# Three decoder blocks on one core: the first mixture's entry is reordered, V rows and table rows of the third mixer move to GpSimd's DMA queue, and the MLA heads are woven another way

## The chip, the cores and the metric

The program runs on one core of a Trainium2 chip. The metric is device time in microseconds (us) of one execution. The median of three runs of the kernel before is the time that a change is measured against. Engines are named as in the profile: PE (TensorE matmul) and PEld (its weight load), DVE (VectorE), ACT (ScalarE), POOL (GpSimd), SP (SyncE). A name with a q (ACTq, POOLq, SPq) is the sequencer of that engine, which issues DMAs in program order.

## The reference

Three blocks follow one another on 512 tokens of width 1024, in fp32. Cut to the parts that the change touches:

```python
def first_block(...):                      # block 1
    mem_n = rms_norm(mem, mem_norm)
    h = h + hybrid_mixer(rms_norm(h, mix_norm), ...)
    h = h + memory_cross_attention(rms_norm(h, cross_norm), mem_n, ...)
    h = h + hierarchical_moe(rms_norm(h, moe_norm), ...)   # 16 experts, top 2
...
def hierarchical_moe(h, w_rg, b_rg, w_re, b_re, w_e_gate, w_e_up, w_e_down):
    g_prob = jax.nn.softmax((hf @ w_rg) + b_rg, axis=-1)
    grp = jnp.argmax(g_prob, axis=-1)
    e_logits = ((hf @ w_re) + b_re).reshape(N, N_GROUPS, EXPERTS_PER_GROUP)
    ...
    top_p, top_i = lax.top_k(jax.nn.softmax(e_logits, axis=-1), TOP_K)
    ...
    u = jax.nn.silu(xb @ w_e_gate[e]) * (xb @ w_e_up[e])     # each expert's own rows
    return u @ w_e_down[e]
```

Block 2 (its own mixer and a mixture of 16 wide experts) lies in the middle of the time and is not touched. Block 3's mixer runs two attentions on one input: a neighbourhood attention of 8 heads of 64 (scores over a window of the 2D grid plus a table of relative positions, softmax, values) and a latent attention (MLA) of 8 heads (scores 512 by 512 of width 96, softmax, values of width 64), then mixes both with gates.

## The kernel before

One core does everything; activations sit transposed in SBUF as a high and a low part, and every dense product takes three matmuls (high by high, high by low, low by high). Weights come from HBM by SP's queue as tiles named `raw`; for each 128 by 512 slice ACT casts the high part `wh` (line 227) and DVE subtracts it to give the low part `wl` (line 230). A Tile layer records the program and places the instructions of each engine in one order; within an engine nothing overtakes, DMA issues included.

**First mixture's entry (block 1).** The last projection of the cross attention ends with four row tiles (`moe1_tile`): sums of squares, `power` (DVE makes `pw_v`, line 215; POOL raises it to the power -1/2, line 216), transposes into `gate` tiles, a small router product (line 912) and the logits `L` (DVE, line 922). `moe1_route` turns the logits into expert lists on DVE: some thirty small operations on tiles `rt`, a cast to bf16 (line 971), count matmuls (lines 975 to 978), then for chunks of experts a one-hot `oh` (line 992), matmuls (line 997) and `token_rows` (lines 1075 to 1078), whose last cast is the integer index. POOL gathers the rows `xe` of each expert with an indirect DMA (line 1132); PE transposes them (line 1088), ACT and DVE split them into `xeh` and `xel`, and the expert's products begin (line 1103). Beside this stand two pieces for block 2: `mem2_keep`, four POOL adds (line 1247), and `mem2_v` for its second half, 48 products (line 428) with eight `wl`.

**Entry of the third mixer.** `dense_tiles` makes V (matmuls of line 376); `ev_v` copies each row tile out of PSUM (DVE, tile `nv`, line 1810) and stores it to DRAM `vd` with a DMA on ACT's queue (line 1811). Then `dense` makes q and k (matmuls of line 428). Eight loads bring V back in windows `vw` (line 1830), and two loads for each pair of heads bring table rows `rv` (line 1839), all on ACT's queue. The neighbourhood attention that follows has scores (1862), softmax, transposes (442) and values (1876).

**MLA heads.** `mla_part(hp, qt)` is one pair of heads and one tile of queries: two scores (line 1968), softmax on DVE and ACT (maximum 462 or 465, exponential 477, reciprocal 482, scale 485), eight transposes (442) with one copy by DVE (445) and one by ACT (447) into `eT`, sixteen value matmuls (1980, in pairs of the two heads) and a copy (1984). Head pair 0 runs earlier; pairs 1 to 3 are run by `stagger(..., 2)`, which keeps two parts open.

```python
self.together([lambda kt=kt, b=b: values(kt, b) for kt in range(4) for b in (1, 0)])
...
stagger((mla_part(hp, qt) for hp in range(1, 4) for qt in range(4)), 2)
```

## Time and profile before

| what | value |
|---|---|
| median of 3 runs | 3352.58 us (3346.15 to 3354.76) |
| profiled execution | 3355.08 us |
| its span | 3353.2 us |
| mean granted TensorE clock | 0.983 |
| busy PE, DVE, ACT, POOL | 3168.3, 1632.4, 1291.2, 130.9 us |

The profile is of one execution. Its span is the time from the first to the last recorded instruction; 1.9 us lie around it. In a timeline row the columns are start, duration, engine, line, operation, tile written from tile read, and count; the bracket at the end is the idle time of that engine just before the row and what ended it. The granted clock (PEclk) is a share of full speed.

### The profile page before, as it was taken

The page shows a single profiled execution, that of the slowest core. Times are in us where ns is not written, and L with a number is a line of the kernel's source. Part 1 is how long each engine was busy: PE and PEld are TensorE (multiplying, and loading weights), DVE is VectorE, ACT ScalarE, POOL GpSimd, SP SyncE. Part 2 cuts the span into 40 slices and gives each one's busy share as a digit, 9 for nine tenths or more (in the row PEclk, how much of TensorE's full clock was granted, in tenths as well). Part 3 has the DMA queues.
Part 4 walks back from the last instruction along what each step waited for, and adds up shares of the span by engine and source line. Part 5 has one row for each costly group of instructions (what it writes and reads, how often), then busy time and mean ns, then how long its engine had stood idle before and what let it go on. Part 6 is the DMA issues. An engine that isn't in the chain of part 4 may idle for free.

```text
span 3353.2 us, 41283 instructions
## 1 busy us (share of the span) xinstructions
PE 3168.3 (94%) x15456; PEld 2062.4 (62%) x15456; DVE 1632.4 (49%) x3520; ACT 1291.2 (39%) x2662; POOL 130.9 (4%) x128
## 2 busy tenths in 40 slices
PE   8999989998989999999999999899888999999998
PEld 6778766667758777677534333322225685788886
DVE  5557799987364444856211111011105546573356
ACT  6335568876354354654000000000003444452244
POOL 0010110001000000000000000000000000000000
PEclk9999989999999999999899999999999999999999
DMA  5115489975112122125799999999995220132243
GB/s 174 67 66 157 173 305 382 370 282 177 63 38 88 63 66 88 39 89 199 315 420 426 427 427 427 427 427 427 427 427 205 72 95 26 63 114 90 81 170 138
DMA packets 196554, 713.96 MB, mean 213 GB/s; under 512 B 20144, under 2 KB 28096, under 8 KB 147584
## 3 DMA queue, kind: packets, MB, share of 16 engines
q1 hardware_dynamic: 173888, 668.38, 51.4%
q10 hardware_dynamic: 19520, 32.43, 3.1%
q0 software_dynamic: 2944, 10.49, 1.0%
q8 instruction: 123, 2.02, 0.2%
q14 instruction: 79, 0.65, 0.1%
HBM read 693.68 MB, written 17.56 MB: 212 GB/s over the span
## 4 chain that ended last, share of the span: by engine, by line
PE 69%; DMA 15%; DVE 8%; ACT 4%; issue 2%; POOL 1%; ACTq 0%; POOLq 0%; SPq 0%; DVEq 0%
PE acc L428 23%; PE acc L291 7%; PE acc L1701 6%; PE acc L1103 5%; PE acc L1295 5%; DMA xl<-in_w_exp_up_dram 3%; DMA rawx<-in_w_exp_gate_dram 3%; PE acc L1738 3%; PE acc L1125 3%; DMA rawx<-in_w_exp_down_dram 2%; DMA xl<-in_w_exp_down_dram 2%; PE sc L1664 2%; PE acc L376 2%; PE pst L442 2%; DVE wl L230 2%
## 5 line engine op out<-in xcount | busy, mean ns | idle before, releaser
L230 DVE TENSOR_TENSOR wl<-raw,wh 128x512 fp32r<-128x512 f32 (+3 forms) x910 | 606.0, 682 | 578.6 <-ACT wh L227 528.9
L227 ACT CAST wh<-raw 128x512 fp32r<-128x512 f32 (+3 forms) x910 | 546.5, 612 | 717.1 <-PE acc L428 475.1
L428 PE MATMUL acc<-xh,wh 128*128 128x512 f32 x1072 | 426.5, 398 | 7.2 <-ACT wh L227 5.2
L428 PE MATMUL acc<-xl,wh 128*128 128x512 f32 x1072 | 424.5, 396 | 0.0
L428 PE MATMUL acc<-xh,wl 128*128 128x512 f32 x1072 | 423.1, 395 | 0.0
L1701 PE MATMUL acc<-rawx,xe 128*64 128x512 f32 x1256 | 293.1, 601 | 28.1 <-DMA rawx<-in_w_exp_up_dram 20.4
L428 PEld LDWEIGHTS acc<-xh,wh 128*128 128x128 f32 x1072 | 202.4, 189 | 57.1 <-ACT wh L227 7.8
L428 PEld LDWEIGHTS acc<-xh,wl 128*128 128x128 f32 x1072 | 202.5, 189 | 47.0 <-issue 6.7
L428 PEld LDWEIGHTS acc<-xl,wh 128*128 128x128 f32 x1072 | 202.7, 189 | 44.2 <-issue 5.6
L1701 PEld LDWEIGHTS acc<-rawx,xe 128*64 128x64 f32 x1256 | 84.4, 137 | 227.5 <-issue 149.8
L1738 PE MATMUL acc<-rawx,wh 128*64 128x512 f32 x640 | 145.9, 598 | 10.6 <-DMA rawx<-in_w_exp_down_dram 10.6
L291 PE MATMUL acc<-wl,xsh 128*128 128x512 f32 x336 | 133.8, 398 | 4.8 <-DVE wl L230 4.7
L216 POOL TENSOR_TENSOR pw_r<-pw_v,halfneg 128x1 f32<-128x1 f32 (+2 forms) x64 | 59.1, 924 | 2008.2 <-DVE pw_v L215 1990.6
L291 PE MATMUL acc<-wh,xsl 128*128 128x512 f32 x336 | 132.9, 396 | 0.0
L291 PE MATMUL acc<-wh,xsh 128*128 128x512 f32 x336 | 128.9, 392 | 0.0
L1701 PE MATMUL acc<-raw,xe 128*64 128x512 f32 x512 | 118.5, 597 | 8.4 <-DMA raw<-in_w_exp_gate_dram 8.4
L1720 DVE SCALAR_TENSOR_TENSOR wl<-wl,acc 128x512 f32<-128x512 f32 x32 | 22.0, 687 | 203.6 <-PE acc L1701 203.6
L1727 ACT COPY wh<-pst 128x512 f32<-128x512 f32 x32 | 18.8, 586 | 259.8 <-PE pst L1726 259.7
L477 ACT ACTIVATE e<-e,smx 128x512 f32<-128x512 f32 (+3 forms) x160 | 98.9, 619 | 50.2 <-DVE smx L475 36.4
L1103 PE MATMUL acc<-wh,xeh 128*96 128x512 f32 x256 | 103.7, 406 | 0.7 <-ACT xeh L227 0.7
L1738 PEld LDWEIGHTS acc<-rawx,wh 128*64 128x64 f32 x640 | 42.7, 136 | 99.2 <-issue 70.7
L1103 PE MATMUL acc<-wl,xeh 128*96 128x512 f32 x256 | 103.5, 404 | 0.1
(537 smaller groups left out, 5475.1 us busy)
## 6 DMA issues: line engine op xcount, KB each, us to landing
rawx<-in_w_exp_up_dram SPq DMA_DIRECT2D x80, 1024.0 KB
rawx<-in_w_exp_down_dram SPq DMA_DIRECT2D x80, 1024.0 KB
rawx<-in_w_exp_gate_dram SPq DMA_DIRECT2D x77, 1024.0 KB
raw<-in_w_in_dram SPq DMA_DIRECT2D x58, 1024.0 KB
raw<-in_w_exp_gate_dram SPq DMA_DIRECT2D x34, 1024.0 KB
raw<-in_w_exp_down_dram SPq DMA_DIRECT2D x32, 1024.0 KB
raw<-in_w_exp_up_dram SPq DMA_DIRECT2D x30, 1024.0 KB
raw<-in_w_ffn_out_dram SPq DMA_DIRECT2D x22, 1024.0 KB
```

The lines of the kernel that those rows point to most:

```text
L227: nc.scalar.copy(hi, src)
L230: nc.vector.tensor_sub(lo, src, hi.bitcast(F32))
L291: nc.tensor.matmul(acc[a, hf], l[:, js], r, start=(k == 0 and q == 0), stop=(k == nk - 1 and q == 2))
L376: self.nc.tensor.matmul(acc[a], l[:, k, js], r[:, :n], start=(k == 0 and q == 0), stop=(k == nk - 1 and q == 2))
L428: nc.tensor.matmul(outs[j], l, r, start=(kk == 0 and q == 0), stop=(kk == nk - 1 and q == 2))
L442: nc.tensor.transpose(pt[:, k * P:(k + 1) * P], src[:, (b + k) * P:(b + k + 1) * P], self.ident)
L477: nc.scalar.activation(es[i], src[i], AF.Exp, bias=nm[:, i:i + 1], scale=sc[i], accum_out=l[:, i:i + 1])
L1103: nc.tensor.matmul(ps, l[:, k], r, start=(k == 0 and q == 0), stop=(k == 7 and q == 2))
L1125: nc.tensor.matmul(py[hf], l[:, k], r, start=(k == 0 and q == 0), stop=(k == 3 and q == 2))
L1295: nc.tensor.matmul(acc[j], l[:, js], r, start=(k == 0 and q == 0), stop=(k == nk - 1 and q == 2))
L1701: nc.tensor.matmul(acc[f // 2][f % 2 * 64:(f % 2 + 1) * 64], cur[:, k, es], raw[f], start=(k == 0), stop=(k == 7))
L1738: nc.tensor.matmul(py[hf * 64:(hf + 1) * 64], uT[ab][:, kk, c * 64:(c + 1) * 64], raw[:, d, hf * 512:(hf + 1) * 512], start=(i + d == 0), ...
```

## The change

Three places change.

1. *First mixture's entry.* `moe1_route` becomes a generator that stops behind its second chunk of indices; `mem2_v` calls it after its fourth slice. `mem2_keep` and `mem2_v` are placed behind the last row tile's `pw_v` and power. The index chunks become (0,1), (1,4), (4,8), (8,12), (12,16), with the second one-hot behind the first index's cast; `keep_busy` adds 15 matmuls of 128 by 512 in bf16 behind the chunks.
2. *Entry of the third mixer.* V's row tiles are staged in tiles `ne` and `neT`; the stores `vd`, the loads `vw` and `rv` are issued by POOL (`nc.gpsimd`) and no longer by ACT. The weight loads of V, q and k are raised to the front; those of k go to a tile `m` of the merge.
3. *MLA heads.* `mla_part` yields once more, and `weave` replaces `stagger`.

```diff
+    def keep_busy(self, ps, b, n, behind):
+        with self.tc.issue_after(behind):
+            for _ in range(n):
+                self.nc.tensor.matmul(ps, b, b.unsqueeze(1).to_broadcast([P, 4, P]), start=True, stop=True)
...
-        for e0, e1 in ((0,2),(2,5),(5,8),(8,12),(12,16)):
+        done = None
+        busy = self.acc()
+        for e0, e1 in ((0, 1), (1, 4), (4, 8), (8, 12), (12, 16)):
+            if e0 == 4:
+                yield
             n = e1 - e0
             oh = self.XS.tile([P, 4, 4, C], BF, name="oh", bufs=2)
...
+            with tc.issue_after(done) if e0 == 1 else ExitStack():
+                nc.vector.tensor_tensor(oh[:, :, :n], ...)
...
+            if e0:
+                self.keep_busy(busy, self.onesb, 3 if e1 < 16 else 6, mm.ins)
+            done = self.token_rows(self.idx[:C, e0:e1], ...)
...
         def ev_v(a, ps):
-            t = N.tile([P, 512], F32, name="nv")
+            t = (N.tile([P, 2, 256], F32, name="ne", bufs=2).rearrange("p i k -> p (i k)") if a % 2 else
+                 N.tile([P, 4, P], F32, name="neT", bufs=2).rearrange("p k t -> p (k t)"))
             nc.vector.tensor_copy(t, ps)
-            nc.scalar.dma_start(vd[a * P:(a + 1) * P, :], t)
+            nc.gpsimd.dma_start(vd[a * P:(a + 1) * P, :], t)
...
+        raws = {c: [self.raw_group(W, kg, 4, c, 512) for kg in (0, 4)] for c in (1024, 0)}
+        for kg in (0, 4):
+            nc.sync.dma_start(room[:, kg:kg + 4], W[kg * P:(kg + 4) * P, 512:1024].rearrange("(g p) n -> p g n", p=P))
...
-                nc.scalar.dma_start(t, bass.AP(tensor=o.tensor, offset=o.offset, ap=[[64 * 512, 4], [512, 32], [1, 512]]))
+                nc.gpsimd.dma_start(t, bass.AP(tensor=o.tensor, offset=o.offset, ap=[[64 * 512, 4], [512, 32], [1, 512]]))
...
-                nc.scalar.dma_start(rv, bass.AP(tensor=rpb.tensor, offset=rpb.offset + (2 * hp + hh) * 945,
+                nc.gpsimd.dma_start(rv, bass.AP(tensor=rpb.tensor, offset=rpb.offset + (2 * hp + hh) * 945,
...
+            scores(0)
+            yield
+            with behind():
+                last[0] = scores(1).ins
             e = H.tile([P, 2, S], F32, name="e", bufs=3)
...
+                last[0] = self.transposes(eT[:, b], e[:, b], 4, eng="a" if b else "v")
+            yield
             po = self.pst() if hp == 0 else self.acc()
...
+            with behind():
+                self.together([lambda kt=kt, b=b: values(kt, b) for kt in range(4) for b in (1, 0)])
...
+        def weave(parts, depth, tied):
+            open_ = []
+            for g in parts:
+                o = open_.pop(0) if len(open_) == depth else None
+                next(g)
+                last[1] = tied and o is not None
+                if o is None or not tied:
+                    next(g)
+                if o is not None:
+                    next(o)
+                    if tied:
+                        next(g)
+                    next(o, None)
+                open_.append(g)
...
-        stagger((mla_part(hp, qt) for hp in range(1, 4) for qt in range(4)), 2)
+        weave([mla_part(hp, qt) for hp in range(1, 4) for qt in range(4)], 2, True)
...
-            self.moe1_route()
-            self.mem2_keep(*m[0])
-            self.mem2_v(*m[0], (1,))
+            last = self.last_power
+            route = self.moe1_route()
+            with tc.issue_after(last[0]), tc.issue_after(last[1]):
+                self.mem2_keep(*m[0])
+                self.mem2_v(*m[0], (1,), lambda: next(route))
+            next(route, None)
```

**Place 1 in the order of DVE.** Before, the last row tiles and the start of the routing: `xs_3863` belongs to the last row tile, `L_2933` is written once for each row tile, and `rt` opens the routing.

```order
L901 TENSOR_TENSOR xs_3863<-h_2450,grow_3551 128x512
L922 SCALAR_TENSOR_TENSOR L_2933<-sc_3889,pw_r_3856,rb_2912 128x20
L230 TENSOR_TENSOR wl_4165<-raw_4152,wh_4164 128x512
L445 COPY gate_3873<-pst_3874 128x512
L230 TENSOR_TENSOR wl_4175<-raw_4152,wh_4174 128x512
L230 TENSOR_TENSOR wl_4185<-raw_4152,wh_4184 128x512
L230 TENSOR_TENSOR wl_4197<-raw_4194,wh_4196 128x512
L215 TENSOR_SCALAR pw_v_3883<-ss_3880 128x1
L230 TENSOR_TENSOR wl_4207<-raw_4194,wh_4206 128x512
L922 SCALAR_TENSOR_TENSOR L_2933<-sc_3899,pw_r_3884,rb_2912 128x20
```

The same place of the changed kernel, where line 221 is the old 215, 932 the old 922 and 237 the old 230:

```order
L221 TENSOR_SCALAR pw_v_3855<-ss_3852 128x1
L911 TENSOR_TENSOR xs_3863<-h_2450,grow_3551 128x512 x2
L454 COPY gate_3845<-pst_3846 128x512
L221 TENSOR_SCALAR pw_v_3883<-ss_3880 128x1
L237 TENSOR_TENSOR wl_3923<-raw_3920,wh_3922 128x512
L237 TENSOR_TENSOR wl_3933<-raw_3920,wh_3932 128x512
L454 COPY gate_3873<-pst_3874 128x512
L932 SCALAR_TENSOR_TENSOR L_2933<-sc_3889,pw_r_3856,rb_2912 128x20
L237 TENSOR_TENSOR wl_3943<-raw_3920,wh_3942 128x512
L237 TENSOR_TENSOR wl_3953<-raw_3920,wh_3952 128x512
L932 SCALAR_TENSOR_TENSOR L_2933<-sc_3899,pw_r_3884,rb_2912 128x20
```

The last `pw_v` moved ahead of four `wl`; four more `wl`, which stood ahead of it or at the end, now stand inside the routing chain behind the last `L`. On POOL the four adds of line 1247 stood ahead of the last power and now stand behind it.

**Place 2 in the orders of ACT and POOL.** Before, on ACT, the casts of q's weights (`wh` from `raw`) and the DMA issues among them:

```order
L227 CAST wh_19083<-raw_19033 128x512
L1811 DMA vd_18779<-nv_19014 128x512
L1830 DMA vw20_19317<-vd_18779 128x1x512
L227 CAST wh_19101<-raw_19099 128x512
L1830 DMA vw30_19321<-vd_18779 128x1x512
L1830 DMA vw01_19311<-vd_18779 128x1x512
L1830 DMA vw11_19315<-vd_18779 128x1x512
L227 CAST wh_19117<-raw_19099 128x512
L1830 DMA vw21_19319<-vd_18779 128x1x512
L1830 DMA vw31_19323<-vd_18779 128x1x512
L1839 DMA rv_19443<-in_na_rpb_3_dram 128x1x489
L227 CAST wh_19133<-raw_19099 128x512
```

In the changed kernel they stand on POOL, in this row (the two powers are those of the last two row tiles of the norm ahead of the mixer):

```order
L1864 DMA rv_19341<-in_na_rpb_3_dram 128x1x489
L222 TENSOR_TENSOR pw_r_18752<-pw_v_18751,halfneg_83 128x1
L222 TENSOR_TENSOR pw_r_18774<-pw_v_18773,halfneg_83 128x1
L1832 DMA vd_18795<-neT_18906 128x512
L1832 DMA vd_18795<-ne_18909 128x512
L1855 DMA vw00_19316<-vd_18795 128x1x512
L1855 DMA vw10_19320<-vd_18795 128x1x512
L1855 DMA vw20_19324<-vd_18795 128x1x512
L1855 DMA vw30_19328<-vd_18795 128x1x512
L1832 DMA vd_18795<-neT_18969 128x512
L1832 DMA vd_18795<-ne_19029 128x512
L1855 DMA vw01_19318<-vd_18795 128x1x512
```

Three more `vw` and six `rv` follow there; ACT's casts stand in a row with no DMA between them. Two `rv` stand between the powers of the second and the third row tile.

**Place 3 in the order of PE.** Before, two parts of head pair 2 (`sc` or two `acc` hold scores, `acc` with `eT` values):

```order
L442 MATMUL pst_21293<-c_ident_81,e_21183 128x128 x4
L442 MATMUL pst_21299<-c_ident_81,e_21183 128x128 x4
L1980 MATMUL acc_21305<-eT_21292,mv_20099 64x128
L1968 MATMUL acc_21315<-mkT_21264,mqT_21257 128x512
L1980 MATMUL acc_21305<-eT_21292,mv_20099 64x128 x7
L1968 MATMUL acc_21316<-mkT_21278,mqT_21271 128x512
L442 MATMUL pst_21330<-c_ident_81,e_21219 128x128 x4
L442 MATMUL pst_21336<-c_ident_81,e_21219 128x128 x4
L1968 MATMUL sc_21352<-mkT_21264,mqT_21257 128x512
L1980 MATMUL acc_21342<-eT_21329,mv_20099 64x128 x8
L1968 MATMUL sc_21352<-mkT_21278,mqT_21271 128x512
```

The same parts in the changed kernel (line 451 is the old 442, 1994 the old 1968, 2012 the old 1980):

```order
L451 MATMUL pst_21290<-c_ident_81,e_21203 128x128 x4
L451 MATMUL pst_21296<-c_ident_81,e_21203 128x128 x4
L1994 MATMUL sc_21287<-mkT_21285,mqT_21278 128x512
L2012 MATMUL acc_21312<-eT_21289,mv_20106 64x128 x8
L1994 MATMUL acc_21322<-mkT_21271,mqT_21264 128x512
L451 MATMUL pst_21326<-c_ident_81,e_21239 128x128 x4
L451 MATMUL pst_21332<-c_ident_81,e_21239 128x128 x4
L1994 MATMUL acc_21323<-mkT_21285,mqT_21278 128x512
L2012 MATMUL acc_21349<-eT_21325,mv_20106 64x128 x8
```

Before, the first value matmul followed right behind the transposes in most parts; now one score always stands between the transposes and the values, and one behind the values.

## Rows read from the trace of the kernel before

**Rows 1.** The page's first part: busy time, share of the span, instructions.
```profile
PE 3168.3 (94%) x15456; PEld 2062.4 (62%) x15456; DVE 1632.4 (49%) x3520; ACT 1291.2 (39%) x2662; POOL 130.9 (4%) x128
```

**Rows 2.** The chain of waits at the third mixer's entry: start, us, what.
```profile
2573.07 11.24 DMA vd<-nv
```

**Rows 3.** Timeline of ACT there: issues held in ACT's queue, and casts.
```profile
2574.90 10.52 ACTq L1830 DMA_DIRECT2D vw<-vd  x3
2585.51 0.62 ACT L227 CAST wh<-raw 128x512 fp32r<-128x512 f32 x1 [10.02 <-DMA vw<-vd]
...
2593.70 2.18 ACT L227 CAST wh<-raw 128x512 fp32r<-128x512 f32 x4 [7.56 <-issue]
```

**Rows 4.** Timeline of PE there: q's products.
```profile
2572.13 0.39 PE L428 MATMUL acc<-xh,wh 128*128 128x512 f32 x1
...
2585.50 0.39 PE L428 MATMUL acc<-xh,wl 128*128 128x512 f32 x1
...
2594.37 0.80 PE L428 MATMUL acc<-xh,wh 128*128 128x512 f32 x1 [4.88 <-ACT wh L227]
...
2600.08 0.46 PE L428 MATMUL acc<-xl,wh 128*128 128x512 f32 x1
```

**Rows 5.** By line, ns min/median/max: POOL's DMA issues, V's evictions, first values.
```profile
L1132 POOL DMA_INDIRECT xe<-hn_d,rt x16: 909/1313/2398, 425.8 to 636.5; - x16
...
DMA to landing us min/median/max: 5.1/8.3/10.2
...
L1810 DVE COPY nv<-acc x4: 681/683/693, 2559.6 to 2572.4; 128x512 f32<-128x512 f32 x4
...
L1876 PE MATMUL pst<-neT,vw x24: 272/273/323, 2630.6 to 2636.8; 128*64 128x128 f32 x24
```

**Rows 6.** Timeline of POOL at the norm ahead of the third mixer.
```profile
2547.04 1.49 POOL L216 TENSOR_TENSOR pw_r<-pw_v,halfneg 128x1 f32<-128x1 f32 x2 [3.05 <-DVE pw_v L215]
```

**Rows 7.** Timeline of PE in the MLA heads 1 to 3.
```profile
2835.96 1.04 PE L442 MATMUL pst<-c_ident,e 128*128 128x128 f32 x8
2837.73 0.43 PE L1980 MATMUL acc<-eT,mv 128*64 128x128 f32 x2 [0.73 <-ACT eT L447]
...
2841.13 1.04 PE L442 MATMUL pst<-c_ident,e 128*128 128x128 f32 x8
...
2844.95 1.04 PE L442 MATMUL pst<-c_ident,e 128*128 128x128 f32 x8
...
2879.71 1.09 PE L1980 MATMUL acc<-eT,mv 128*64 128x128 f32 x16 [0.73 <-ACT eT L447]
```

**Rows 8.** Waits from 2800 to 2885: engine, line, waited for: us in total, times, longest.
```profile
PE acc L1980 <- ACT eT L447: 7.1, 10, 0.7
```

**Rows 9.** Window there: PE, PEld, DVE, ACT, POOL busy (count), PEclk, DMA share, GB/s.
```profile
2840.00:2850.00 10.00, 9.32 (x62) 5.37 (x59) 7.36 (x17) 5.29 (x14) 0.00 (x0) 1.00 0.01 2
```

**Rows 10.** Timeline of DVE at the first mixture's entry.
```profile
408.65 1.64 DVE L230 TENSOR_TENSOR wl<-raw,wh 128x512 fp32r<-128x512 f32 x1
...
414.20 0.14 DVE L215 TENSOR_SCALAR pw_v<-ss 128x1 f32<-128x1 f32 x1
414.27 0.67 DVE L230 TENSOR_TENSOR wl<-raw,wh 128x512 fp32r<-128x512 f32 x1
...
420.03 0.19 DVE L971 CAST rt<-rt 128x64 bf16<-128x64 f32 x1
...
425.29 0.17 DVE L1078 CAST rt<-trf 96x2 int32<-96x2 f32 x1
...
438.45 1.02 DVE L230 TENSOR_TENSOR xel<-pst,xeh 128x384 fp32r<-128x384 f32 x2
```

**Rows 11.** Timeline of POOL at the same place.
```profile
408.48 1.27 POOL L1247 TENSOR_TENSOR gate<-memh,meml 128x512 f32<-128x512 f32 x1 [0.39 <-PE sc L912]
...
414.49 0.86 POOL L216 TENSOR_TENSOR pw_r<-pw_v,halfneg 128x1 f32<-128x1 f32 x1 [0.76 <-DVE pw_v L215]
```

**Rows 12.** Window at the same place, columns as in group 9.
```profile
430.00:435.00 5.00, 2.01 (x11) 1.64 (x11) 4.43 (x25) 0.22 (x1) 1.87 (x2) 0.50 0.83 232
```

More of the change, by code (lines that the diff above doesn't have):

```diff
@@ L214, in power @@
         r = self.small.tile([P, 32], F32, name="pw_r")
-        self.nc.vector.tensor_scalar(v[:, :n], ss, 1.0 / width, eps, op0=OP.mult, op1=OP.add)
-        self.nc.gpsimd.tensor_tensor(r[:, :n], v[:, :n], self.halfneg[:, :n], op=OP.pow)
+        a = self.nc.vector.tensor_scalar(v[:, :n], ss, 1.0 / width, eps, op0=OP.mult, op1=OP.add)
+        b = self.nc.gpsimd.tensor_tensor(r[:, :n], v[:, :n], self.halfneg[:, :n], op=OP.pow)
+        self.last_power = [a.ins, b.ins]
         return r
@@ L430, in dense @@
             k += g
+            if mid is not None and k == 4:
+                mid()
         for j in range(nj):
@@ L996, in moe1_route @@
                 for a in range(4):
-                    nc.tensor.matmul(px[:C, e * 2:e * 2 + 2], oh[:, a, e], tokb[:, a], start=(a == 0), stop=(a == 3))
-            self.token_rows(self.idx[:C, e0:e1], px[:C, :2 * n].rearrange("p (e v) -> p e v", v=2), R)
+                    mm = nc.tensor.matmul(px[:C, e * 2:e * 2 + 2], oh[:, a, e], tokb[:, a], start=(a == 0),
+                                          stop=(a == 3))
+            if e0:
+                self.keep_busy(busy, self.onesb, 3 if e1 < 16 else 6, mm.ins)
+            done = self.token_rows(self.idx[:C, e0:e1], px[:C, :2 * n].rearrange("p (e v) -> p e v", v=2), R)
         ex = T(4, 4)
@@ L1077, in token_rows @@
                                             op1=OP.add)
-        self.nc.vector.tensor_copy(out, f[:self.C, :n])
+        return self.nc.vector.tensor_copy(out, f[:self.C, :n]).ins
     def moe1_gemm(self, M, xe, gate, up, down, out):
@@ L1279, in mem2_v @@
             self.dense(I["w_mem_kv_2"], 8, 1024 + c * 512, 512, "N", mh, ml,
-                       lambda j, ps: nc.scalar.copy(self.v2[:, j, c * 512:(c + 1) * 512], ps), ntok=256)
+                       lambda j, ps: nc.scalar.copy(self.v2[:, j, c * 512:(c + 1) * 512], ps), ntok=256,
+                       mid=mid)
     def denseT_f32(self, W, nk, c0, x, evict):
@@ L1800, in mixer3 @@
         o_ml = [B.tile([P, S], F32, name=f"oml{i}") for i in range(4)]
-        merged = [B.tile([P, S], F32, name=f"m{i}") for i in range(8)]
+        room = B.tile([P, 8, S], F32, name="m")
+        merged = [room[:, i] for i in range(8)]
         self.g8 = B
@@ L1808, in ev_v @@
         def ev_v(a, ps):
-            t = N.tile([P, 512], F32, name="nv")
+            t = (N.tile([P, 2, 256], F32, name="ne", bufs=2).rearrange("p i k -> p (i k)") if a % 2 else
+                 N.tile([P, 4, P], F32, name="neT", bufs=2).rearrange("p k t -> p (k t)"))
             nc.vector.tensor_copy(t, ps)
-            nc.scalar.dma_start(vd[a * P:(a + 1) * P, :], t)
-        self.dense_tiles(W, 8, 1024, 512, xh, xl, ev_v)
+            nc.gpsimd.dma_start(vd[a * P:(a + 1) * P, :], t)
+        raws = {c: [self.raw_group(W, kg, 4, c, 512) for kg in (0, 4)] for c in (1024, 0)}
+        for kg in (0, 4):
+            nc.sync.dma_start(room[:, kg:kg + 4], W[kg * P:(kg + 4) * P, 512:1024].rearrange("(g p) n -> p g n", p=P))
+        raws[512] = [room[:, kg:kg + 4] for kg in (0, 4)]
+        self.dense_tiles(W, 8, 1024, 512, xh, xl, ev_v, raws=raws[1024])
         anti = self.const("anti", N)
@@ L1966, in mla_part, with scores @@
             sp = self.sc() if hp == 0 or qt % 2 == 0 else [self.acc(), self.acc()]
-            for b in range(2):
-                nc.tensor.matmul(sp[b] if isinstance(sp, list) else sp[:, b], T[2 * b][:96, qt * P:(qt + 1) * P],
-                                 T[2 * b + 1][:96], start=True, stop=True)
+            def scores(b):
+                return nc.tensor.matmul(sp[b] if isinstance(sp, list) else sp[:, b],
+                                        T[2 * b][:96, qt * P:(qt + 1) * P], T[2 * b + 1][:96], start=True, stop=True)
+            scores(0)
+            yield
+            with behind():
+                last[0] = scores(1).ins
             e = H.tile([P, 2, S], F32, name="e", bufs=3)
@@ L1974, in mla_part @@
             for b in range(2):
-                self.transposes(eT[:, b], e[:, b], 4, eng="a" if b else "v")
+                last[0] = self.transposes(eT[:, b], e[:, b], 4, eng="a" if b else "v")
+            yield
             po = self.pst() if hp == 0 else self.acc()
@@ L1981, in values, with behind @@
                                         start=(kt == 0), stop=(kt == 3))
-            self.together([lambda kt=kt, b=b: values(kt, b) for kt in range(4) for b in (1, 0)])
+            with behind():
+                self.together([lambda kt=kt, b=b: values(kt, b) for kt in range(4) for b in (1, 0)])
             nc.scalar.copy(o_ml[hp][:, qt * P:(qt + 1) * P], po[:, :P])
         heads = {}
-        stagger(mla_part(0, qt) for qt in range(4))
+        last = [None, False]
+        def behind():
+            return tc.issue_after(last[0]) if last[1] else ExitStack()
+        def weave(parts, depth, tied):
[12 more added lines that the diff above has]
+                open_.append(g)
+            last[1] = False
+            for g in open_:
+                next(g)
+                next(g, None)
+        weave([mla_part(0, qt) for qt in range(4)], 1, False)
         for hf in range(2):
```

17 lines of the change are left out of this document (9 added, 8 removed).

## Prediction

> **What bounds the kernel now.** I read the page's first part, then the chain of waits, the timelines and the windows at the three places that the diff touches. PE is busy for 94% of the span [rows 1], so an edit gains only where PE stands still or runs at its half clock, and I look for those stretches. There are three.
>
> At the third mixer's entry the chain of waits leaves PE for a DMA: the store of V's last row tile takes 11.24 us [rows 2]. Three loads of V's windows, queued behind it on ACT, sit there for 10.52 us, and ACT's next cast, which stands behind them in program order, comes 10.02 us late; a second cast comes 7.56 us late, behind two more window loads and a table load [rows 3]. The second delay reaches PE: it idles 4.88 us before the matmul at 2594.37, and the matmuls behind it are long until 2600.08 [rows 4]. PE needed none of those transfers; it waited for a cast held up in the queue of the engine that issued them.
>
> In the MLA heads 1 to 3 PE waits ten times for ACT's copy of `eT`, 7.1 us in all [rows 8]. It happens where the first value matmul follows directly behind the transposes [rows 7].
>
> At the first mixture's entry DVE is the binder: from the last row tile's `pw_v` at 414.20 through the routing to the first expert's `xel` at 438.45 [rows 10] PE has little to do, 2.01 us of 5 with the clock at 0.50 in one window [rows 12].
>
> **The change part by part.**
>
> *Third mixer's entry, what goes.* ACT loses its DMA issues, so its casts follow each other. From 2572.13 to 2585.50 PE started 60 products, 59 steps of 0.2266 us [rows 4]. The product at 2600.08 is the 86th. Without the hole it would start at 2572.13 + 85 x 0.2266 = 2591.4. The gain is **8.7 us**, some 5.5 of idle time and the rest slow matmuls. PE bounds what follows, so I let all of it through.
>
> *What comes: twenty DMAs on POOL.* Their price on POOL isn't in the trace; the nearest rows are the indirect gathers, 0.91 to 2.40 us each with a median of 1.31, landing after 8.3 us (up to 10.2) [rows 5]. A plain store should be no dearer, and I take 1.3. POOL is nearly idle [rows 1], but its queue also runs in order. There, two stores are followed by four loads that wait for their landing, then the other two stores and four loads. The first evictions are done by about 2563.3 [rows 5]; with p for one DMA and 11.2 us for a store's landing [rows 2] the first four loads are through POOL at 2574.5 + 5p, the last loads have been issued at 2585.7 + 11p and land 8.9 us later (my value inside the gathers' span), at 2594.6 + 11p. The first value matmul, at 2630.6 before [rows 5], comes 8.7 us earlier; the order puts table matmuls and scores behind the k copies, about 2.5 us later than now, so I put the need at 2624.4. At p = 1.3 the loads land at 2609 and nobody waits; at p = 2.4 they land at 2621, still in time. A wait begins at p = 2.7. Below that the edit costs nothing on PE, since remaining q and k products cover it.
>
> *The queues passed.* Two table loads now stand on POOL ahead of the power of row tile 2. POOL idled 3.05 us before that power [rows 6]; 2 x 1.3 fits, 2 x 2.4 would be 1.8 us too long. I take 0, with 2 as the end. SP's queue keeps its order; the k weights only land in other tiles.
>
> The Trainium skill (SBUF — State Buffer, "A bandwidth-pool intuition that's wrong") speaks against this move: a DMA issued from GpSimd that takes about 620 ns alone takes about 3100 ns beside a DVE copy, because its descriptors wait for a port. As an estimate from that page, p = 3.1 gives a landing at 2628.7 and a delay of 4.3 us, so 4.4 of the 8.7 us would be left. No plain DMA on POOL is in the trace of before; the gathers' longest, 2.40, lies nearer to it than their median does.
>
> *MLA heads.* The order puts one score between the transposes and all sixteen values in each part. The trace has both forms. From one part's transposes to the next it takes 2841.13 - 2835.96 = 5.17 us with the wait, and 2844.95 - 2841.13 = 3.82 us in the part where a score stood there [rows 7]: 1.35 us. Ten waits stand in the stage [rows 8]; the last two, the last of them at 2879.71 [rows 7], stay, because no scores are left to put there. That makes 8 x 1.35 = 10.8. ACT now meets the copy behind exponentials in its queue at times; I take off 0.3 for that: **10.5 us**. Can softmax follow at 3.82? In the window from 2840 to 2850, which holds about 2.3 parts, DVE is busy 7.36 and ACT 5.29 [rows 9], so some 3.2 and 2.3 us for a part. Both fit, DVE without much room. Ends: 4 if DVE's order costs half a microsecond and more in each of twelve parts, 13 if the half-clock start of the stage shortens too.
>
> *First mixture's entry.* Four `wl` leave the front of the last `pw_v`: 1.64 us for the first of them while a POOL add runs (408.48 to 409.75), 0.67 for one beside no add [rows 10, 11]. The last `pw_v` can then come near 407.5, some 6.7 us earlier. Most of that is given back: four `wl` now lie inside the routing chain (4 x 0.67 = 2.7), and the four adds, behind the last power, run beside the routing operations of two SBUF inputs and may hold each up to 1.3 us [rows 11]. From the bf16 cast to the first index it is 425.29 - 420.03 = 5.26 us now [rows 10]; with a one-hot for one expert, and the next behind the index's cast, about 3.6, a gain of 1.7. The rest to `xel` (438.45 - 425.29 = 13.2) keeps gather, transposes and split. I put `xel` at 434.7 to 437.2, so 1.2 to 3.7 us earlier, and take **2 us**. The fifteen extra matmuls stand in PE's idle time; as they hold the clock, the half-speed products behind 439 might gain up to 2 us, and as fewer products stand ahead of the routing, 3 may be lost. Ends: -3 and +6.
>
> The Trainium skill (SBUF — State Buffer, "Who interferes with whom") has the mechanism: a DVE instruction with two SBUF inputs contends with a GpSimd instruction that reads SBUF, and the one that is first keeps the port for its whole instruction. The stretched `wl`, 1.64 against 0.67 [rows 10], agrees with it. It speaks against putting the adds beside the routing, and the first rival is that.
>
> **Sum.** 8.7 + 10.5 + 2 = 21.2 us. Against the profiled run, 3355.1, that is 3333.9; it stands 2.5 us above the median of 3352.6, which gives **3331**. With the ends of the terms the forecast's own range is 3322 to 3341.
>
> **The rivals.**
>
> *One: the entry of the mixture loses.* The adds hold the routing chain for 4 x 1.3 = 5 us and the four `wl` add 2.7; with the index's 1.7 and 6.7 from the front the balance is about zero, and 3 us below it if the clock falls earlier. This also covers the case that the change doesn't do what its words say, the clock not being held. 3352.6 - 8.7 - 10.5 + 0 to 3 = 3333 to 3336. For it: the stretched `wl`. Against: the routing operations are short, and most of an add's time passes on waits.
>
> *Two: softmax becomes the bound of the MLA heads.* DVE's 3.2 of 3.82 us leaves little; if a maximum sits behind an `eT` copy in each part, 4 us of the 10.5 remain, and with nothing at the mixture: 3352.6 - 8.7 - 4 = 3340. Against: the part of 3.82 us was run with no wait for softmax.
>
> *Three, the slower side: POOL's queue is the new wait.* Eleven DMAs in series decide: each further microsecond of p is 11 us of delay. At p = 4 the values come 14.2 us late: 3345.6. At 5.6 the delay of 31.8 us takes the whole 21.2 and 10.6 more: 3363, slower than before. For it: gathers of 2.40 us, and DVE splitting weights all along. Against: their median is 1.31. The page named above would put p at 3.1, 3336, which is on the forecast's side.
>
> **How the numbers follow.** Forecast 0.60. Rival one 0.15, all faster. Rival two 0.12, of it 0.04 within the bound. Rival three 0.10: 0.06 within, 0.04 slower. The rest, 0.03, I split into 0.02 within and 0.01 slower. A difference of 0.3%, 10 us here, is about what a measurement of this kernel can tell from none, so faster means below 3342.5: 0.60 + 0.15 + 0.08 = 0.83; same 0.12; slower 0.05. Leaving out the lowest part of the forecast and the upper half of rival three, the range is 3321 to 3345.
>
> **What would show it.** At the third mixer's entry: no idle row of PE before a product of q, twenty DMA rows on POOL of 1 to 2.4 us, and no wait of values for `vw`; a wait for `vw` there speaks for rival three. In the MLA heads: no waits of the values for `eT` but the last two and a step of 3.8 us; waits of PE for `e` or of the transposes for DVE speak for rival two. At the mixture: the first `xel` 1 to 4 us earlier, counted from the end of the cross attention's products; long routing rows beside POOL's adds speak for rival one. What would make the prediction wrong as a whole is a transfer or a buffer that I have taken as covered: `ne` and `neT`, which now hold V until its store has landed, or PE's cold stretches moving elsewhere.

## The result and the profile after

The changed kernel takes **3327.42 us** (median of 4 runs, 3325.39 to 3331.5) against 3352.76 us (4 runs, 3346.15 to 3354.76) for the kernel before on the same chip: a ratio of 0.9929, interval 0.9912 to 0.9947, or 25.3 us less by the medians. The same kernel timed a second time among the experiments gave 3331.27 (5 runs) against 3349.3 (15 runs), 0.9945 (0.9931 to 0.9959), or 18.0 us less. The direction and the size (3331 predicted, 3321 to 3345) held; two of the reasons did not.

The first part of the page of after answers to [rows 1]: DVE and ACT do the same work, PE is 14 us less busy, POOL 14 us more.

```profile
PE 3153.9 (95%) x15471; PEld 2055.1 (62%) x15471; DVE 1634.3 (49%) x3520; ACT 1291.3 (39%) x2662; POOL 145.3 (4%) x148
```

To see where the time went I cut each profiled run at PE rows that every kernel has (the last product of the cross attention, the first down product of the first mixture, the end of each mixture, the first transposes of MLA head pair 0 in the third mixer, the last MLA values). Each cell is the difference of two start times, in us:

| kernel | cross attention to first down product | to the end of mixture 1 | to mixture 2, nothing changed | mixture 2, nothing changed | to the first transposes of MLA head pair 0 | to the last MLA values | to the end |
|---|---|---|---|---|---|---|---|
| before | 54.3 | 285.4 | 865.7 | 924.8 | 232.4 | 115.0 | 472.7 |
| after | 51.3 | 285.3 | 861.7 | 924.7 | 224.1 | 101.0 | 472.4 |
| after, second time | 51.3 | 285.5 | 865.9 | 924.3 | 224.1 | 101.0 | 472.3 |
| e1, entry alone | 51.2 | 285.2 | 865.4 | 924.8 | 232.6 | 113.5 | 472.7 |
| e2, third mixer alone | 54.3 | 285.4 | 865.3 | 925.0 | 224.9 | 110.6 | 472.4 |
| e3, heads alone | 53.3 | 285.3 | 865.5 | 924.4 | 230.4 | 99.4 | 472.5 |
| e4, no extra matmuls | 53.1 | 287.0 | 865.9 | 924.7 | 224.3 | 101.1 | 472.3 |
| e5, matmuls alone | 57.0 | 286.9 | 865.6 | 924.7 | 232.7 | 109.0 | 472.6 |
| e6, queue alone | 54.3 | 285.6 | 866.1 | 924.3 | 234.5 | 110.6 | 472.4 |
| e7, staging alone | 54.2 | 285.5 | 865.1 | 924.6 | 232.5 | 115.0 | 472.6 |
| e8, gather early | 53.1 | 287.1 | 863.7 | 923.9 | 224.7 | 100.9 | 472.5 |
| e10, nine matmuls | 53.9 | 285.3 | 863.3 | 924.6 | 224.1 | 101.0 | 472.5 |
| e11, ACT, loads late | 53.3 | 285.3 | 863.3 | 924.0 | 231.5 | 113.5 | 472.7 |

The table has its own noise. Code that no kernel changed takes 861.7 to 866.1 us in the third column, 923.9 to 925.0 in the fourth, 472.3 to 472.7 in the last; the stretch ahead of the first column, which no kernel changed either, takes 400.0 to 405.0. Against the profiled run of before, after gains 3.0 us at the first mixture, 8.3 at the third mixer and 14.0 in the MLA heads, 25.3 in all; against the mean of all kernels that have the old code in the place (before, e2, e3, e6, e7, e11: 339.4; before, e1, e3, e5: 232.0; before, e1, e2, e5, e6, e7, e11: 112.5) it gains 2.8, 7.9 and 11.5, or 22.2. The 4.0 us that its first profiled run shows in the third column did not come back the second time (865.9) and are chance.

**Third mixer's entry.** The window of 20 us behind V's last eviction has no gap left, where [rows 4] show a hole of 4.88 us (columns as in [rows 9]). ACT's casts come at a regular step, behind PE's release of their buffers and behind no issue, where [rows 3] had 10.02 and 7.56.

```profile
2564.40:2584.40 20.00, 20.00 (x90) 16.57 (x89) 6.12 (x10) 5.18 (x10) 3.28 (x5) 1.00 1.03 278
```
```profile
2566.29 0.62 ACT L234 CAST wh<-raw 128x512 fp32r<-128x512 f32 x1 [1.87 <-PE acc L435]
2569.01 0.62 ACT L234 CAST wh<-raw 128x512 fp32r<-128x512 f32 x1 [2.10 <-PE acc L435]
```

POOL's timeline has the DMAs that ACT lost: four stores at 0.56 to 0.63 us, eight loads in two groups of 2.7 us.

```profile
2553.80 0.63 POOL L1832 DMA_DIRECT2D vd<-neT  x1 [13.33 <-DVE neT L1831]
2554.41 0.56 POOL L1832 DMA_DIRECT2D vd<-ne  x1
2557.58 2.74 POOL L1855 DMA_DIRECT2D vw<-vd  x4 [2.60 <-DMA vd<-ne]
2560.31 0.59 POOL L1832 DMA_DIRECT2D vd<-neT  x1
2565.37 0.56 POOL L1832 DMA_DIRECT2D vd<-ne  x1 [4.46 <-DVE ne L1831]
2573.89 2.73 POOL L1855 DMA_DIRECT2D vw<-vd  x4 [7.96 <-DMA vd<-ne]
```

**MLA heads.** Answering to [rows 7], PE's timeline runs transposes, a score, sixteen values, a score without a gap; only the last two parts wait for `eT`. The step from transposes to transposes is 3.81 us in the rows shown. The second fence is the list of waits, answering to [rows 8] (7.1, ten times).

```profile
2834.33 1.04 PE L451 MATMUL pst<-c_ident,e 128*128 128x128 f32 x8
2835.20 1.02 PE L1994 MATMUL acc<-mkT,mqT 96*128 96x512 f32 x2
2836.16 1.09 PE L2012 MATMUL acc<-eT,mv 128*64 128x128 f32 x16
...
2838.14 1.04 PE L451 MATMUL pst<-c_ident,e 128*128 128x128 f32 x8
...
2847.25 1.09 PE L2012 MATMUL acc<-eT,mv 128*64 128x128 f32 x16 [1.33 <-ACT eT L456]
...
2850.10 1.09 PE L2012 MATMUL acc<-eT,mv 128*64 128x128 f32 x16 [0.73 <-ACT eT L456]
```
```profile
PE acc L2012 <- ACT eT L456: 2.1, 2, 1.3
```

**First mixture's entry.** DVE's timeline answers to [rows 10]: the last `pw_v` at 406.80 (414.20 before), the bf16 cast at 419.82 (420.03), the first index at 423.20 (425.29), the first `xel` at 437.05 (438.45). So 7.4 us of lead have shrunk to 0.2 at the cast. Two `wl` and one routing operation are long while POOL adds.

```profile
406.80 0.14 DVE L221 TENSOR_SCALAR pw_v<-ss 128x1 f32<-128x1 f32 x1
...
408.81 2.71 DVE L237 TENSOR_TENSOR wl<-raw,wh 128x512 fp32r<-128x512 f32 x2
...
412.74 1.24 DVE L956 TENSOR_TENSOR rt<-rt,c_first 128x16 f32<-128x16 f32 x1
...
419.82 0.20 DVE L981 CAST rt<-rt 128x64 bf16<-128x64 f32 x1
...
423.20 0.14 DVE L1096 CAST rt<-trf 96x1 int32<-96x1 f32 x1
423.26 3.01 DVE L1007 TENSOR_TENSOR oh<-c_iota,rt 128x1152 bf16<-128x1152 f32 x2
...
437.05 0.55 DVE L237 TENSOR_TENSOR xel<-pst,xeh 128x384 fp32r<-128x384 f32 x1
```

POOL's timeline (answering to [rows 11]) has the four adds, and the first gather, whose issue alone takes 5.45 us beside the next one-hots:

```profile
407.92 6.03 POOL L1265 TENSOR_TENSOR gate<-memh,meml 128x512 f32<-128x512 f32 x4
423.65 5.45 POOL L1150 DMA_INDIRECT xe<-hn_d,rt  x1 [9.70 <-DVE rt L1096]
```

The windows from 430 to 445, answering to [rows 12]: PE has work nearly throughout, but its granted clock is 0.50 here too and only rises from 435 on. Before, the two later windows had 0.50 and 0.70.

```profile
430.00:435.00 5.00, 5.00 (x29) 2.80 (x29) 2.67 (x21) 0.00 (x0) 2.59 (x3) 0.50 0.79 245
435.00:440.00 5.00, 4.47 (x21) 3.02 (x20) 4.67 (x18) 2.58 (x5) 0.91 (x1) 0.90 0.47 143
440.00:445.00 5.00, 5.00 (x23) 3.49 (x22) 4.99 (x9) 4.64 (x9) 0.00 (x0) 1.00 0.37 134
```

### The profile page after: what moved, and what is told of

It is laid out like the page before. It is cut to its first block, busy times and chain, and to the rows that moved or that the text cites. A ratio compares the mean times of both kernels' runs of the same rounds, so it can differ in the third digit from the quotient of the medians.

```text
span 3323.3 us, 41342 instructions
## 1 busy us (share of the span) xinstructions
PE 3153.9 (95%) x15471; PEld 2055.1 (62%) x15471; DVE 1634.3 (49%) x3520; ACT 1291.3 (39%) x2662; POOL 145.3 (4%) x148
## 4 chain that ended last, share of the span: by engine, by line
PE 55%; DMA 11%; DVE 6%; ACT 3%; issue 1%; POOL 1%; ACTq 0%; POOLq 0%; SPq 0%; DVEq 0%
PE acc L435 20%; PE acc L1720 8%; PE acc L298 5%; PE acc L1314 5%; PE acc L1757 4%; DMA rawx<-in_w_exp_gate_dram 4%; DMA xl<-in_w_exp_up_dram 3%; DMA xl<-in_w_exp_down_dram 2%; PE sc L1683 2%; ACT e L487 2%; PE pst L1766 1%; PE pst L451 1%; DMA rawx<-in_w_exp_down_dram 1%; PE acc L383 1%; DVE e L478 1%
## 5 line engine op out<-in xcount | busy, mean ns | idle before, releaser
L237 DVE TENSOR_TENSOR wl<-raw,wh 128x512 fp32r<-128x512 f32 (+1 forms) x902 | 600.3, 682 | 554.7 <-ACT wh L234 505.1
L234 ACT CAST wh<-raw 128x512 fp32r<-128x512 f32 (+1 forms) x902 | 542.6, 612 | 691.5 <-PE acc L435 466.5
L1314 PE MATMUL acc<-wl,wh 128*128 128x512 f32 x256 | 102.0, 398 | 1.0 <-DVE wl L237 1.0
```

Of the source, the lines that this page charges most:

```text
L234: nc.scalar.copy(hi, src)
L237: nc.vector.tensor_sub(lo, src, hi.bitcast(F32))
L1314: nc.tensor.matmul(acc[j], l[:, js], r, start=(k == 0 and q == 0), stop=(k == nk - 1 and q == 2))
```

## The experiments

### Each place alone: e1, e2, e3

**e1** is the kernel before with the changed entry of the first mixture (router, `keep_busy`, `mid`); **e2** the kernel before with the new staging of V, the raised loads and POOL's queue; **e3** the kernel before with `weave` (which runs head pair 0 too, where nothing moved: from its first transposes to those of pair 1 it is 41.2 to 41.3 us in every kernel).

> The kernel before with the change at the first mixture's entry alone. Theory, read from the changed kernel's trace (last expert product of this mixture 3.1 us earlier): 3 us faster than before, of which 1.4 us is the first xel product starting earlier and 1.7 us is that the expert's first products run at the full clock. Rival (POOL's adds and the four wl inside the routing chain give it all back): 0 us. Second rival (the 4.2 us that the changed kernel gained between 1458 and 1608 us, in code that no edit touches, is caused by this entry and not by chance of the clock): 7 us.

> The kernel before with the change at the third mixer's entry alone (V staged in ne and neT, loads raised, vd, vw and rv issued by POOL). Theory: ACT's casts are no longer held, PE's hole of 4.88 us and the slow products behind it go: 8.7 us faster, no idle of PE before a product of q, DMA rows on POOL of 0.6 to 0.7 us. Rival (POOL's queue is the new wait): values wait for vw, gain under 4 us.

> The kernel before with the change of the MLA heads alone. Theory: 10.5 us from eight waits of the values for eT, each worth 1.35 us, and 3.5 us more because the stage's first parts, at half clock before, run at the full clock: 14 us faster, steps of 3.82 us from part to part, waits for eT only before the last two groups of values. Rival (the clock in the first parts differs from run to run and was luck in the profiled run): 10.5 us.

| run | median | before | ratio (interval) |
|---|---|---|---|
| e1 | 3348.04 | 3350.27 | 0.9991 (0.9981 to 1.0001) |
| e2 | 3343.23 | 3350.27 | 0.998 (0.997 to 0.9989) |
| e3 | 3339.93 | 3350.27 | 0.9971 (0.9959 to 0.9982) |

The differences, 2.2, 7.0 and 10.3 us, add up to 19.6; the whole change gave 18.0 and 25.3. So no action of one place on another shows within this noise. In e1's trace the third column (865.4) is that of before, so its second rival falls. For e3 14 us were expected and 10.5 by its rival; the time gives 10.3. In e3 the stage has two waits for `eT` (1.33 and 0.73) and a step of 3.82 us, as in after. In e2 the DMA rows of POOL take 0.56 to 0.74 us each and no value waits for `vw`: rival three falls. This holds although DVE splits weights and copies out of PSUM almost without pause while POOL issues the first two stores and four loads, as the window of e2 shows (DVE 18.57 of 20 us):

```profile
2550.00:2570.00 20.00, 20.00 (x97) 16.57 (x96) 18.57 (x29) 14.89 (x25) 4.51 (x7) 1.00 0.18 46
```

### The queue without the staging: e6, and the staging without the queue: e7

The prediction gave the whole gain to ACT's queue. e6 moves the DMAs and keeps the tile `nv`; e7 keeps ACT's queue and takes the new tiles and raised loads.

```
e6:
             nc.vector.tensor_copy(t, ps)                  # t is still nv, one buffer
-            nc.scalar.dma_start(vd[a * P:(a + 1) * P, :], t)
+            nc.gpsimd.dma_start(vd[a * P:(a + 1) * P, :], t)
     (vw and rv likewise)
e7:
-            t = N.tile([P, 512], F32, name="nv")
+            t = (N.tile([P, 2, 256], F32, name="ne", bufs=2)... if a % 2 else
+                 N.tile([P, 4, P], F32, name="neT", bufs=2)...)
     (and raws=..., all DMAs still nc.scalar)
```

> The kernel before with the queue alone swapped at the third mixer's entry: stores vd and loads vw and rv are issued by POOL, V is staged in nv as before and no load is raised. Theory (ACT's casts held behind DMAs are the whole loss): the stretch from block 2's last product to the first transposes of MLA head pair 0 is 224 to 226 us in place of 232, 6 to 8 us faster. Rival (staging and raised loads carry part of it): 228 us or more.

> The kernel before with V staged in ne and neT and the loads raised, but all DMAs on ACT's queue as before. Theory: the hole stays, since casts still stand behind loads that wait for stores: 230 to 233 us for the same stretch, 0 us. Rival: 224 to 226 us.

e6 gave 3351.36 against 3351.23, 1.0009 (0.9999 to 1.0019); e7 gave 3350.27, 1.0002 (0.9991 to 1.0012). Neither half gains anything. In e6 no cast is held up by an issue any more, but the hole is still there with another releaser. Two of the waits of e6 from 2515 to 2620 (engine, line, waited for: us, times, longest):

```profile
DVE nv L1810 <- DMA vd<-nv: 9.5, 1, 9.5
PE acc L428 <- DVE nv L1810: 8.6, 1, 8.6
```

POOL's timeline of e6 says why. There is one `nv`, so the fourth eviction waits until the third store has landed, and on POOL that store follows two loads of `vw`. It was issued at 2566.76 and DVE got the tile back at 2579.36, 12.6 us later; in before the third store was issued at 2567.00 and the fourth `nv` was written at 2572.36 without a wait.

```profile
2565.35 1.41 POOL L1830 DMA_DIRECT2D vw<-vd  x2 [2.69 <-PE acc L376]
2566.76 0.59 POOL L1811 DMA_DIRECT2D vd<-nv  x1
...
2580.34 0.59 POOL L1811 DMA_DIRECT2D vd<-nv  x1 [11.04 <-DVE nv L1810]
```

DVE stands in `nv` for 9.5 us and PE waits 8.6 us for it. In after a store lands 2.4 to 12.2 us after its issue, no sooner than in e6 (2.4 to 12.5), but each of the four tiles is used once and nobody waits. The weight loads raised in e2 and after, and not in e6, were not tried apart from the tiles; the wait itself is one for `nv`. In e7 the other half of the old hole remains, ACT held up by its own queue:

```profile
ACT wh L227 <- DMA rv<-in_na_rpb_dram: 15.9, 1, 15.9
PE acc L428 <- ACT wh L227: 6.2, 1, 6.2
```

### ACT's queue, with the loads behind the last copy of q: e11

Is POOL needed, or would ACT do if its loads came later, when there is no store to wait for? e11 is e7 with the loads of `vw` and `rv` placed behind ACT's fourth `nq` copy.

```
-                nc.scalar.dma_start(t, bass.AP(tensor=o.tensor, ...
+                with tc.issue_after(nq[3]):
+                    nc.scalar.dma_start(t, bass.AP(tensor=o.tensor, ...
     (rv likewise)
```

> The kernel before with V staged in ne and neT and the loads raised, all DMAs on ACT's queue, but the window loads and the table loads placed behind the last q copy, so that no cast of q's weights stands behind a load that waits for a store. POOL issues none of them. Theory (the loss was casts held behind waiting loads, and with two staging tiles for V any queue that holds no cast will do): 5 to 7.5 us faster than before, 225 to 228 us from block 2's last product to the first transposes of MLA head pair 0. Rival (POOL's queue is needed): 230 us or more, 0 to 2 us.

3349.54 against 3349.3, 0.9998 (0.9989 to 1.0007): nothing, where 5 to 7.5 us had been expected. ACT's timeline of e11 shows the issues themselves lasting, and casts of k's weights held behind them. The second fence is PE's longest wait in e11 from 2515 to 2640:

```profile
2591.34 7.18 ACTq L1838 DMA_DIRECT2D vw<-vd  x3
2598.62 0.62 ACT L227 CAST wh<-m 128x512 fp32r<-128x512 f32 x1 [6.66 <-issue]
2598.64 5.21 ACTq L1848 DMA_DIRECT2D rv<-in_na_rpb_dram  x2
2603.96 0.62 ACT L227 CAST wh<-m 128x512 fp32r<-128x512 f32 x1 [4.71 <-issue]
```
```profile
PE pst L1851 <- DMA rv<-in_na_rpb_dram: 4.7, 1, 4.7
```

Three loads hold ACT for 7.18 us and two table loads for 5.21; four of the same window loads took POOL 2.73 in after, with no cast behind them. Why ACT's issues are that long is not shown by these rows. But PE lost nothing to the late casts: it has no wait for a cast here beyond 0.3 us of a weight load, and q's products run without a hole. It lost 4.7 us, and some slow products behind them, to the table rows: e11 issued their loads at 2598.64, behind the last copy of q and the long issues of the window loads, while after issued its first two at 2536.56, ahead of V. So e11 does not show that POOL's queue is needed. ACT's queue with the window loads late and the first table loads early was not tried, and stays a rival.

### The extra matmuls: e4, e5, e10

e4 is after without the fifteen `keep_busy` matmuls, e10 after without the last six of them; e5 is the kernel before with all fifteen. None of their results is read.

```
e4:
-            if e0:
-                self.keep_busy(busy, self.onesb, 3 if e1 < 16 else 6, mm.ins)
e10:
+            if 0 < e0 < 12:
+                self.keep_busy(busy, self.onesb, 3, mm.ins)
```

> The changed kernel without its fifteen extra matmuls (keep_busy left out; they write to a tile that nothing reads). Theory (the clock is their gain): PE idles between the index chunks, the first expert's products start at the half clock, 1 to 2 us slower than the changed kernel. Rival (they do nothing for the clock and stand ahead of the transposes of xe, which start only when the last of them ends): 0 to 2 us faster than the changed kernel.

> The kernel before with the fifteen extra matmuls alone, behind its own index chunks (they write to a tile that nothing reads). Theory (the extra matmuls carry all of the entry's 3 us, by the clock of the first expert's products; without them the reordering gained nothing): 2 to 3 us faster than before, the stretch from the cross attention's last product to the first down product 51.5 to 52.5 us in place of 54.3. Rival (the extra matmuls only pay together with the reordering, which leaves PE idle later): 0 us, 54.3.

> The changed kernel without the last six of the fifteen extra matmuls, so that nothing but index matmuls stands ahead of the transposes of the first expert's rows. Theory (those six stand on the path, 2.7 us at half clock, and the clock rises at about the same moment with real products in their place): the transposes start at about 432.6 in place of 435.2, 1 to 2.5 us faster than the changed kernel. Rival (the clock then stays low for the first expert, as without any of the fifteen): 2 to 4 us slower than the changed kernel.

| run | median | before | ratio (interval) |
|---|---|---|---|
| e4 | 3331.42 | 3350.27 | 0.9943 (0.9929 to 0.9958) |
| e10 | 3328.59 | 3349.3 | 0.9941 (0.9927 to 0.9955) |
| after, second time | 3331.27 | 3349.3 | 0.9945 (0.9931 to 0.9959) |
| e5 | 3357.34 | 3351.23 | 1.0024 (1.0014 to 1.0033) |

> The changed kernel once more, beside the next one on the same chip. Theory (the three places give 3.0, 7.4 and 12.5 us; 4 us of the profiled run's 29.9 us fell in code that no edit touches, between 742 and 1608 us, and were chance of the clock): 23 us faster than before, that same stretch 865 to 866 us. Rival (the stretch was shortened by the change): 25 us or more, 862 us again.

For after the second time 23 us had been expected; the time gives 18.0, and its third column is 865.9, as expected. In whole times e4, e10 and after can't be told apart. In the traces they can. PE's timelines of after and of e4: in e4 the transposes come 2.8 us sooner, since in after the last six extra matmuls stand ahead of them, and the first product with `xel` 1.0 sooner (437.65 in after), but products at 0.63 us run until 442.7; in after they take 0.39 from 437.96 on.

```profile
432.64 2.72 PE L208 MATMUL acc<-onesb 128*128 128x512 bf16 x6
435.15 1.26 PE L1106 MATMUL pst<-c_ident,xe 96*128 96x96 f32 x8
...
437.96 0.39 PE L1121 MATMUL acc<-wh,xeh 128*96 128x512 f32 x1
```
```profile
432.38 1.51 PE L1103 MATMUL pst<-c_ident,xe 96*128 96x96 f32 x8 [1.02 <-DVE rt L1046]
...
436.61 0.74 PE L1118 MATMUL acc<-wh,xel 128*96 128x512 f32 x1 [1.62 <-DVE xel L237]
437.15 0.63 PE L1118 MATMUL acc<-wh,xeh 128*96 128x512 f32 x1
...
442.70 0.42 PE L1118 MATMUL acc<-wl,xeh 128*96 128x512 f32 x1
442.96 0.39 PE L1118 MATMUL acc<-wh,xel 128*96 128x512 f32 x1
```

e10 looks like e4, as its rival had it: its transposes start at 430.85, but the first expert's products take 0.63 us until 441.06, and where after has a granted clock of 0.90 (435 to 440) e10 has 0.50:

```profile
435.00:440.00 5.00, 3.74 (x9) 2.54 (x10) 3.10 (x10) 1.64 (x3) 0.00 (x0) 0.50 0.26 75
```

Counted from the cross attention's last product, the expert's products come down to 0.39 us after some 35 us in after (both times) and e1, and after some 40 us in before, e4 and e10. In the first column of the table the old entry has 53.3 to 54.4, e4 53.1, e10 53.9, and the whole entry 51.2 to 51.3. (e4 loses another 1.6 us in the second column: over the last 7.8 us of the mixture its clock was 0.78, that of before 1.00.) So in these traces the reordered entry without the matmuls, or with nine of them, gains 1.3 us at most, and the 3 us come only with all fifteen, by the clock. That is one profiled run of e4 and of e10 and three of the whole entry, and the times don't confirm it: e10's median is the lowest in the table above. It stays open.

e5 is slower, which neither its theory nor its rival had, but it is no clean test: with the matmuls in, the order of PE changed as well. Some forty memory products now stand between the index matmuls and the transposes, which start at 443.05, and PE idles through 415 to 420.

```profile
415.00:420.00 5.00, 0.00 (x0) 0.00 (x0) 4.55 (x26) 0.42 (x2) 1.25 (x1) 0.50 0.76 240
```

### The first gather sooner: e8

After's first gather takes 5.45 us to issue. e8 issues it at once, holds the next one-hot until it is out (a one-column POOL write stands between), puts the second half of the memory's products where PE would then idle, and raises their weight loads.

```
+            if e0 == 0:
+                g0 = self.gather(self.xe0[:C], self.hn_d, self.idx[:C, 0:1]).ins
+            if e0 == 1:
+                with tc.issue_after(g0):
+                    nc.gpsimd.memset(oh[:, 0, 0, :1], 0.0)
     (and the memory's slices 4 to 7 behind the first index matmuls)
```

> The changed kernel with three more edits at the first mixture's entry: the first expert's gather is issued as soon as its index is there, the next one-hot waits until POOL has issued it, and the memory products of slices 4 to 7 with their wl stand behind that one-hot and no longer inside the routing chain. Theory (POOL's issue of the first gather, 5.45 us in the changed kernel and 0.91 where no one-hot ran beside it, is held by DVE; four wl of 0.68 lengthen the chain): the gather's issue takes 0.9 to 1.2 us, the first xel product comes 3 to 6 us earlier, 3 to 5 us faster than the changed kernel. Rival (PE's order and the clock decide, since the extra matmuls of the last chunk still stand ahead of the transposes): within 2 us of the changed kernel.

```profile
422.22 1.35 POOL L1166 DMA_INDIRECT raw<-hn_d,rt  x1 [7.71 <-DVE rt L1079]
```
```profile
425.14 1.12 PE L1022 MATMUL pst<-b_tok,oh 128*96 128x2 bf16 x12 [3.06 <-DVE oh L1015]
...
438.49 0.83 PE L1122 MATMUL pst<-c_ident,raw 96*128 96x96 f32 x8
```

The gather is out after 1.35 us, at 423.57, where after has 429.10. Yet PE's timeline has the transposes at 438.49 (after: 435.15): PE waits 3.06 us for the one-hot that was held back, and the transposes stand behind the memory's products and all the index matmuls. 3331.63 against 3351.23, 0.995 (0.9937 to 0.9962), is the ratio of after. In the first column of the table e8 has 53.1, as e4 has. So a short issue of the gather brings nothing by itself: behind it PE's own order bounds e8, and in after the extra matmuls stand there.

## Why the prediction was right or wrong

**Third mixer's entry: size right, cause half right.** 8.7 was forecast; 8.3 came in after, 7.5 in e2 against before, 7.0 in the time of e2. The hole was the right one, and the price on POOL lies below the lower end that the prediction took (0.56 to 0.74 against 0.91; 1.3 was its value). The Trainium skill (SBUF — State Buffer, "A bandwidth-pool intuition that's wrong") has 3.1 us for such a DMA beside a DVE copy. The rows don't show it: none of the twenty DMAs was stretched, though DVE was busy for 18.57 of 20 us around the first stores and loads; its copies there read PSUM, and none from SBUF to SBUF ran beside those. The step that failed is "ACT loses its DMA issues, so its casts follow each other": it credits the queue alone. The casts do follow each other in e6, but the move makes a new wait of the same length, and it is gone where V has four tiles (e2, after). The prediction had the pieces: it wrote that on POOL two stores are followed by four loads and then the other two stores, and it put 11.2 us on a store's landing. With one `nv` this is a wait of DVE (9.5 us in e6); it had named `ne` and `neT` only as something that could hold V, when it is the old tile that does. That the size came out so near is in part luck: the queue that was credited with all of it gains nothing alone.

**MLA heads: mechanism right, a second gain counted only as an end.** Eight of ten waits went, the last two stayed, the step is 3.82 us. The term of 10.5 measured 14.0 between the two profiled runs, 11.5 against the mean of the old code, 10.3 in the time of e3. From the transposes of head pair 1's q and k to the first product behind the stage the old order took 73.97, 72.43, 69.58, 72.45 and 67.91 us (before, e1, e2, e11, e5), the new one 59.93, 59.92 (after, twice) and 58.30 (e3). What separates the old ones is the clock of the second ten us: 0.50, 0.55, 0.86, 0.56 and 1.00; in the new order it was 0.83, 0.84 and 1.00. The two rows are those of before and of after:

```profile
2816.80:2826.80 10.00, 9.32 (x30) 4.94 (x29) 4.54 (x10) 2.20 (x6) 0.00 (x0) 0.50 0.01 2
```
```profile
2801.20:2811.20 10.00, 9.22 (x63) 5.83 (x61) 6.85 (x15) 4.67 (x13) 0.00 (x0) 0.83 0.00 0
```

At like clock the order alone is worth 69.58 - 59.93 = 9.7 us (e2 and after, 0.86 and 0.83) and 67.91 - 58.30 = 9.6 (e5 and e3, both 1.00), a little under the 10.5; of the missing part 0.6 is the last wait but one, 1.33 us in place of 0.73. The half-clock start costs the old order 0 to 6.1 us (73.97 - 67.91), and of the 14.0 between the two profiled runs 4.4 are its (73.97 - 69.58). The prediction had this as its upper end of 13. What sets that clock isn't shown; it need not be chance, for the seven profiled runs with POOL's queue in the third mixer had 0.83 to 0.90, and those with ACT's 0.50 to 0.56 or 1.00. Rival two falls: neither DVE nor ACT became the bound.

**First mixture's entry: size near, mechanism not the one argued.** 2 was forecast, 3.0 came in the trace of after, 3.1 in that of e1; the time of e1 gives 2.2, with no change inside its interval. `xel` is 1.4 us earlier, inside the 1.2 to 3.7, and `pw_v` came at 406.80 where 407.5 was said. Three steps fail. "Most of that is given back" falls short: four `wl` and the held operations left 0.2 us of the lead at the bf16 cast. And "the rest to `xel` keeps gather, transposes and split" left out that a one-hot started right behind the first index holds the gather's issue, 5.45 us in place of 2.40 before. "The fifteen extra matmuls stand in PE's idle time" isn't so for the last six: they stand ahead of the first expert's transposes for 2.7 us, and without them (e4) those start that much sooner. The gain seen in the trace comes with the clock of the first expert's products (0.90 against 0.50 in one window), which the prediction had as a term of up to 2 us and then didn't count; that the 2 us lie near is luck. Rival one is near to e4's trace (340.1 us over the first two columns, 339.7 before), but not to what after did.

**The sum.** 21.2 us were forecast; the places give 22.2 to 25.3 in the traces, and the two measurements of the time 25.3 and 18.0. These two differ by more than any of the corrections above, so how near 3331 lies to 3327 and 3331 says nothing finer than some 4 us of time, or 7 us of gain. The forecast's own range, 3322 to 3341, is not what its ends add up to: 8.7 + 13 + 6 gives 3324.9, and 8.7 - 2 + 4 - 3 gives 3344.9.

## What to carry to other kernels

Where an engine stands behind a transfer, ask before moving the transfer who else waits for its landing: a single buffer that was free in time on the old queue can be the next wait of the same length on the new one, and then only the move and more buffers together bring the gain. Where such a move is undone piece by piece, look for what PE waits for in each piece: e11 lost its gain to table loads that came too late, a wait that neither before nor after has. DMAs that wait for other DMAs don't belong in the queue of an engine whose computing PE waits for; an idle engine's queue takes them for about 0.7 us each. Where matmuls wait for a copy of what was just transposed, put other matmuls between the two, and read the step from the place in the trace where this happens already.

## What the runs showed of the hardware

- An indirect gather's issue on POOL lasted 0.91 us in quiet, 2.40 in before, 5.45 in after and 1.35 where the next one-hot was held back (e8; its second gather then took 5.86), while plain DMAs of POOL stayed at 0.56 to 0.74 beside DVE's work. The one-hots have two SBUF inputs. The Trainium skill (SBUF — State Buffer, "Who interferes with whom") says that such a DVE instruction contends with a GpSimd instruction that reads SBUF; the gather's indices lie there, and these rows agree. Which of the two held which, and why 5.45, isn't shown.
- ACT's issue of a few loads in a row held ACT for 5 to 7 us (e11) where POOL issued four of the same in 2.7.
- The same code gets its full clock at different times in different kernels: the second ten us of the MLA stage had 0.50 to 1.00 in five kernels with the same code there, worth 6.1 us, and untouched code between the mixtures took 861.7 to 866.1 us.
